# Forms of an input made by VectorE alone over three gate tiles, more convolution taps inside the attention, and the last pair's products in another order

## The chip, the cores and the metric

The kernel runs on one core of a Trainium2 chip. A core has a matrix engine (TensorE, PE in the profile, with its weight loads shown as PEld), a vector engine (VectorE, DVE), a scalar engine (ScalarE, ACT), a general engine (GpSimd, POOL) and a queue that issues DMAs (SyncE, SP). The metric is the device time of one launch, in microseconds (us), as a median of runs. Time before: 1506.61 us, median of 3 runs (1505.62 to 1508.06).

## The reference

One step of a streaming encoder layer. 1024 prompt frames and 32 sample frames (1056 columns in all, width 1024) are normalised, projected into nine column ranges of one matrix, and go through two branches that are mixed by gates:

```python
h = rmsnorm(x, norm_g)                      # (1056, 1024)
q, k, v, logf, ga, ua, ub, gb, ma, mb = column ranges of h @ w_in
q, k = per-head rmsnorm;  logf = log_sigmoid(logf + b_f);  c = cumsum(logf)
o = softmax(q k^T + c_q - c_k, causal) v    # 16 heads of 64; sample frames see 512 cached keys
u = ua * sigmoid(ub)
conv = causal depthwise convolution of u, 31 taps per channel, + b_dw
ya = (o * silu(ga)) @ w_pa
yb = (silu(layernorm(conv)) * silu(gb)) @ w_pb
m = sigmoid(ma) * ya + sigmoid(mb) * yb
y = x + m @ w_out
```

The keys, values, log gates and the last 30 rows of u are outputs too.

## The kernel before

Everything is laid out with channels on the 128 partitions and the 1056 columns along them, in eight tiles of 128 channels. All arithmetic is 32-bit: an operand is split into a high part (rounded, made on ScalarE) and a low part (the rest, made on VectorE or GpSimd), and a product is three matmuls, high by high, low by high, high by low. A projection tile is 128 output channels by three slices of 352 columns, 8 depth tiles each, so 24 steps of 3 matmuls (`steps`, L109 holds the matmuls). Its weights come by DMA as `raw` (L90), and are split into `wh` on ScalarE (L98) and `wl` on GpSimd (L101).

The stages follow one another:

1. Normalisation and transposition of the input, channels 0 to 3 of u, the values, then q and k (`qk`), whose rounded parts are stored to HBM in slices (L743 to L746, tiles `qh`, `ql`).
2. Attention, 16 heads by 8 blocks of 128 queries, plus four blocks for the sample frames. Only TensorE's order is as written; the other engines are ordered by a scheduler. The loop starts the scores three blocks ahead of the block whose weights are transposed (`turn`), and the weighted values come two blocks later (`values`). Between them `fill(4)` takes four steps of projections from a list, `FILLS`: u 4 to 7, ga 1 to 7, ma 0 to 5 (504 steps). They use one PSUM bank, `pq`.
3. The rest of ma (tiles 6 and 7), over which the forms (below) are made. From here to the end of the pairs TensorE, VectorE and ScalarE execute in the written order, in which `later(n, f)` places a piece of work n beats behind, a beat being a step of 3 matmuls.
4. gb and mb, 16 tiles in eight pairs. A pair of tiles is computed with seven products instead of eight (`Pair`, Strassen's scheme in Winograd's form, L1117 the matmuls, 24 per product). The input's halves in depth and columns are combined into the forms `xf` (three of them: index 1, 2 and 0) and a fourth, called `third` in the code, which is written over the input's own high and low parts once those are no longer needed as they were. The weights are combined per pair into `sa` and `sb` by VectorE (`made`, L1091 to L1099) and split (L1077 ScalarE, L1080 GpSimd). Seven products go to four PSUM tiles a, b, c, d; products 4, 5 and 6 reuse a, c and d once they have been evicted (`evac`, L1127 to L1145; product 0 and 4 on ScalarE, the others on VectorE).
5. The attention's output times silu(ga), called halves here (`a_half`, eight of them: two loads, an activation, a product, a high and a low part), then the projection pa, the convolution's layernorm beside it, pb and out.

The convolution is 31 taps per channel tile: the first on ScalarE, thirty on VectorE (L273, 240 in all). They stand in a list, `taps`. At each beat `pace["credit"]` grows by a rate and taps are taken while the credit allows; evictions and `made` charge it. The rates are `R_A` = 0.12 in the attention and `R_S` = 0.17 in the pairs; the gate tiles of stage 3 start with a credit of -9. At the beginning of the last pair whatever is left is issued at once, and the memory of the convolution is given to the tiles of the halves:

```python
            elif i == 0:
                pump(len(taps))
                pcv.close()
                pap = ExitStack()
                bg = pool("bg", 5, stack=pap, side="right")
            elif i in (3, 4):
                later(2, lambda i=i: (a_half(2 * i - 6), a_half(2 * i - 5)))
```

The forms in stage 3 are made so: GpSimd adds the high and low part of two input tiles (`form_adds`, L1015), VectorE adds a third, and subtracts (L1033, L1035, L1040), ScalarE rounds (L1022), VectorE makes the low parts (L1025). Two of the four tiles of form 0 and half of `third` are made during pair 0 (`fourth_adds`, `third_sums`, `third_form`, `third_low`, L1172 to L1177).

## Time and profile before

| | |
|---|---|
| median of 3 runs | 1506.61 us (1505.62 to 1508.06) |
| the profiled execution: time, span | 1510.4 us, 1508.6 us |
| granted clock, mean | 0.959 |
| TensorE busy | 1386.0 us, 92% |
| VectorE busy | 996.0 us, 66% |
| ScalarE, GpSimd busy | 653.5 us and 652.6 us, 43% each |
| DMA | 201.28 MB, 133 GB/s over the span |

Busy times of the profile are unions of an engine's instructions. The slices are fortieths of the span, 37.7 us each, and a digit is a tenth. In rows with "x", the number behind it counts instructions; in groups the three parts after the count are busy time, mean ns of one, and idle time before it with the engine and line that ended it. A wait row says who waited for whom: total, times, longest.

### The profile page before, as it was taken

Reading aid. Unit: us, or ns where it says so; the run is one execution under the profiler, and the core shown is the slowest. Engines: PE = TensorE matmul, PEld = TensorE weight load, DVE = VectorE, ACT = ScalarE, POOL = GpSimd, SP = SyncE. Lnnn points to the kernel's source line nnn. Section 1 sums busy time; section 2 is a strip of 40 time slices with the busy share of each in tenths; the row PEclk is TensorE's granted clock in tenths of the full one; section 3 lists DMA queues with packets and bytes.
Section 4 is the critical chain, followed back from the end, with each engine's and each line's share of the span. In section 5 each row is a group of like instructions: output and inputs, shape, how many; then the busy total and the mean of one; then the engine's idle time right before and its main releaser. Section 6 shows DMA issues by size and latency. Waiting matters only on the chain.

```text
span 1508.6 us, 25287 instructions
## 1 busy us (share of the span) xinstructions
PE 1386.0 (92%) x9574; PEld 1339.5 (89%) x9574; DVE 996.0 (66%) x1348; ACT 653.5 (43%) x1310; POOL 652.6 (43%) x694
## 2 busy tenths in 40 slices
PE   8999999999999999999999996699970489999999
PEld 7999999998999999999999986699970478999999
DVE  6788788887726666767666676848999677433211
ACT  6333336665655555555555562322210365522100
POOL 3333346675744443443533334656730135545321
PEclk9999999999999999999999998799995689999999
DMA  4353423566344434544545321133310577734531
GB/s 169 115 178 113 160 88 126 172 178 203 140 144 120 143 103 137 154 120 121 155 114 155 110 77 66 48 114 122 103 53 14 201 242 257 235 128 143 161 106 49
DMA packets 107274, 201.28 MB, mean 133 GB/s; under 512 B 16080, under 2 KB 67152, under 8 KB 107152
## 3 DMA queue, kind: packets, MB, share of 16 engines
q1 hardware_dynamic: 107008, 199.60, 41.9%
q8 instruction: 76, 1.25, 0.4%
q14 instruction: 46, 0.38, 0.1%
q10 hardware_dynamic: 144, 0.07, 0.0%
HBM read 129.78 MB, written 69.84 MB: 132 GB/s over the span
## 4 chain that ended last, share of the span: by engine, by line
PE 79%; DVE 10%; DMA 4%; issue 3%; ACT 2%; POOL 1%; SPq 0%; DVEq 0%; POOLq 0%; ACTq 0%
PE pj L109 48%; PE ps L1117 9%; PE pjv L607 6%; DVE y L273 4%; PE ptr L971 4%; PE po L987 3%; PE po L988 2%; PE psS L943 2%; PE psS L944 2%; DMA s_ya<-sma 1%; DMA s_k<-qh 1%; POOL wl L101 1%; DVE t L1015 1%; PE psS L946 1%; DVE y L1358 1%
## 5 line engine op out<-in xcount | busy, mean ns | idle before, releaser
L109 PE MATMUL pj<-xh,wh 128*128 128x352 f32 (+3 forms) x1152 | 387.0, 336 | 14.9 <-ACT t L765 14.4
L109 PE MATMUL pj<-xl,wh 128*128 128x352 f32 (+3 forms) x1152 | 373.2, 324 | 0.2 <-DVE xl L455 0.2
L273 DVE SCALAR_TENSOR_TENSOR y<-u,vec_t,y 128x1086 f32<-128x1086 f32 x240 | 367.0, 1530 | 8.0 <-ACT y L270 5.1
L109 PE MATMUL pj<-xh,wl 128*128 128x352 f32 (+3 forms) x1152 | 372.2, 323 | 0.1
L101 POOL TENSOR_TENSOR wl<-raw,wh 128x384 fp32r<-128x384 f32 (+1 forms) x210 | 242.5, 1183 | 193.8 <-ACT wh L98 171.9
L109 PEld LDWEIGHTS pj<-xh,wh 128*128 128x128 f32 x1152 | 218.3, 189 | 19.2 <-ACT t L765 16.1
L109 PEld LDWEIGHTS pj<-xh,wl 128*128 128x128 f32 x1152 | 218.9, 190 | 0.6 <-POOL wl L101 0.5
L109 PEld LDWEIGHTS pj<-xl,wh 128*128 128x128 f32 x1152 | 217.8, 189 | 1.4 <-DVE xl L455 1.4
L954 POOL TENSOR_SCALAR P<-P,nm 128x128 f32<-128x128 f32 (+7 forms) x128 | 99.6, 778 | 220.9 <-DVE nm L953 179.5
L109 PE MATMUL pj<-ah,wh 128*128 128x352 f32 x768 | 187.8, 327 | 6.6 <-ACT wh L98 6.6
L1117 PE MATMUL ps<-xh,wh 128*128 128x264 f32 x256 | 76.7, 300 | 74.0 <-DVE t L1145 65.3
L109 PEld LDWEIGHTS pj<-ah,wh 128*128 128x128 f32 x768 | 136.1, 192 | 7.3 <-ACT wh L98 7.2
L948 DVE TENSOR_REDUCE nm<-psS 128x1 f32<-128x128 f32 (+7 forms) x128 | 96.7, 756 | 56.1 <-PE psS L946 52.1
L109 PE MATMUL pj<-ah,wl 128*128 128x352 f32 x384 | 125.7, 327 | 8.1 <-POOL wl L101 8.0
L975 ACT CAST pth<-ptr 128x512 fp32r<-128x512 f32 (+1 forms) x192 | 88.8, 481 | 91.0 <-PE ptr L971 90.7
L976 DVE TENSOR_TENSOR ptl<-ptr,pth 128x512 fp32r<-128x512 f32 (+1 forms) x192 | 103.5, 552 | 30.0 <-ACT pth L975 27.1
L1117 PEld LDWEIGHTS ps<-xh,wh 128*128 128x128 f32 x256 | 51.7, 202 | 74.7 <-issue 65.5
L98 ACT CAST wh<-raw 128x1024 fp32r<-128x1024 f32 x70 | 73.4, 1048 | 93.2 <-PE pj L109 85.4
L951 ACT ACTIVATE P<-psS,nm 128x128 f32<-128x128 f32 (+7 forms) x128 | 95.3, 745 | 29.9 <-DVE nm L948 25.6
L744 POOL TENSOR_TENSOR ql<-qn,qh 128x352 fp32r<-128x352 f32 (+1 forms) x48 | 56.6, 1179 | 72.4 <-ACT qh L743 56.4
L971 PE MATMUL ptr<-ident,P 128*128 128x128 f32 x576 | 85.4, 275 | 1.3 <-DVE ptl L976 1.3
L109 PEld LDWEIGHTS pj<-ah,wl 128*128 128x128 f32 x384 | 73.8, 192 | 10.0 <-POOL wl L101 9.9
(245 smaller groups left out, 3040.6 us busy)
## 6 DMA issues: line engine op xcount, KB each, us to landing
raw<-wf SPq DMA_DIRECT2D x88, 512.0 KB
s_v<-vb SPq DMA_DIRECT2D x32, 256.0 KB
QB<-s_q SPq DMA_DIRECT2D x32, 256.0 KB
KB<-s_k SPq DMA_DIRECT2D x32, 256.0 KB
V<-s_v SPq DMA_DIRECT2D x16, 512.0 KB
kT<-qn SPq DMA_DIRECT2D x8, 528.0 KB
s_ga<-t SPq DMA_DIRECT2D x24, 176.0 KB
s_ma<-t SPq DMA_DIRECT2D x24, 176.0 KB
```

The costliest lines, as they stand in the source:

```text
L98: nc.scalar.copy(wh, raw)
L101: nc.gpsimd.tensor_sub(wl[:, k0:k1, :], raw[:, k0:k1, :], f32(wh[:, k0:k1, :]))
L109: nc.tensor.matmul(ps, a[:, kt, :], b(kt, sl), start=(first and n == 0), stop=(last and n == N - 1))
L273: t = nc.vector.scalar_tensor_tensor(y, u[:, i:i + CW], w, y, op0=ALU.mult, op1=ALU.add)
L607: nc.tensor.matmul(ps[:, :VC], a, b, start=(n == 0), stop=(n == 23))
L948: nc.vector.tensor_reduce(nm[:, 0:1], ps[:, :nb, :w], axis=AX.XY, op=ALU.max, negate=True)
L951: nc.scalar.activation(P[:, :nk].rearrange("p (b w) -> p b w", b=nb), ps[:, :nb, :w], AF.Exp, bias=nm[:, 0:1], accum_out=nm[:, 1:2])
L954: nc.gpsimd.tensor_scalar(P[:, :nk], P[:, :nk], nm[:, 2:3], 1.0, op0=ALU.mult, op1=ALU.mult)
L971: nc.tensor.transpose(pt[:, 128 * j:128 * j + 128], P[:, 128 * (4 * u + j):128 * (4 * u + j) + 128], ident)
L975: nc.scalar.copy(pth[:, js, qo], p3)
L976: nc.vector.tensor_sub(ptl[:, js, qo], p3, f32(pth[:, js, qo]))
L1117: nc.tensor.matmul(ps[:, c, :HC], a[:, k, :], x, start=(i < 4 and kt == 0 and n == 0), stop=(kt == 3 and n == 2), skip_group_check=(i >= 4))
```

## The change

It has four parts.

**Taps.** `R_A` goes to 0.18 and `R_S` to 0.27; stage 3 starts with a credit of -24 and pair 0 takes 3 instead of 8 off it.

**Gate tiles and forms.** ma 6 and 7 join `FILLS` (552 steps). A block with index 7 of each head isn't followed by filler. What is left of the list when the attention ends is run then, in the written order, with its PSUM tiles taken from `pq` and the attention's `psT` in turn. Over these steps all forms, the fourth tiles and `third` too, are made by VectorE and ScalarE; GpSimd makes none. `third` is kept in the tiles `sb` and `raw`, which are made larger for it.

**The last pair.** Its products come in the order 0, 1, 2, 3, 5, 6, 4. Halves 0 to 5 are loaded into the tiles `sa`, `sb` and the two `raw` and made between the products; halves 6 and 7 follow in the old way. The weights of pa's first tile are loaded beside product 6.

**Smaller ones.** Three buffers in place of two for `qh` and `ql`; the first head's load stands behind the last key projection; `ones` lies in another pool.

```diff
-R_U, R_V, R_QK, R_S, R_A = 0.25, 0.17, 0.19, 0.17, 0.12
+R_U, R_V, R_QK, R_S, R_A = 0.25, 0.17, 0.19, 0.27, 0.18
...
-         ("ma", 0), ("ma", 1), ("u", 7), ("ma", 2), ("ma", 3), ("ma", 4), ("ma", 5)]
+         ("ma", 0), ("ma", 1), ("u", 7), ("ma", 2), ("ma", 3), ("ma", 4), ("ma", 5),
+         ("ma", 6), ("ma", 7)]
...
-            qh = tp.tile([128, CH], F32R, name="qh", tag="qh")
-            ql = tp.tile([128, CH], F32R, name="ql", tag="ql")
+            qh = tp.tile([128, CH], F32R, name="qh", tag="qh", bufs=3)
+            ql = tp.tile([128, CH], F32R, name="ql", tag="ql", bufs=3)
...
+    class FillBanks:
+
+        n = 0
+
+        def tile(self, *a, **k):
+            self.n += 1
+            if "drain" not in sides or self.n % 2:
+                return pq.tile(*a, **k)
+            return psT.tile([128, 512], F32, name="pj", tag="T")[:, :CH]
...
-    def form_adds(j):
-        part[j] = x32(nc.gpsimd, j, 1), x32(nc.gpsimd, j + 4, 1)
-
-    def form_sums(j, fourth):
-        b12, b22 = part[j]
+    def form_sums(j):
+        b12 = x32(nc.vector, j, 1)
         b11 = x32(nc.vector, j, 0)
         nc.vector.tensor_sub(b11, b12, b11)
         high_of(1, j, b11)
+        b22 = x32(nc.vector, j + 4, 1)
+        nc.vector.tensor_sub(third[j], b22, b12)
         nc.vector.tensor_sub(b22, b22, b11)
         high_of(2, j, b22)
         part[j] = b11, b22
-        if fourth:
-            b21 = x32(nc.vector, j + 4, 0)
-            nc.vector.tensor_sub(b21, b21, b22)
-            high_of(0, j, b21)
-            part[j] = b11, b22, b21
+
+    def form_fourth(j):
+        b21 = x32(nc.vector, j + 4, 0)
+        nc.vector.tensor_sub(b21, b21, part[j][1])
+        high_of(0, j, b21)
+        part[j] += b21,
...
+    def third_high():
+        for j in range(4):
+            nc.scalar.copy(xh[:, j, HT:], third[j])
+
+    def third_low():
+        for j in range(4):
+            nc.vector.tensor_sub(xl[:, j, HT:], third[j], f32(xh[:, j, HT:]))
...
             b.turn()
-            fill(4)
+            if b.i < 7:
+                fill(4)
...
-    pace["credit"] = -9.0
+    pairs = [Pair(k) for k in range(len(SPAIRS))]
+    pace["credit"] = -24.0
...
+    later(39, first_loads)
     for j in range(4):
-        later(9 * j + 2, lambda j=j: form_sums(j, j < 2))
...
+        third[j] = t3[:, (j % 2) * HT:(j % 2) * HT + HT]
+        later(18 * j + 2, lambda j=j: form_sums(j))
+        later(18 * j + 7, lambda j=j: form_fourth(j))
+        later(18 * j + 12, lambda j=j: form_lows(j))
+    for i, at in enumerate((48, 57, 60)):
         later(at, lambda i=i: pairs[0].made(i))
-    later(44, lambda: third_sums((0, 1), nc.gpsimd))
-    for f in (6, 7):
-        for _ in gate_steps("ma", f, pjB):
-            pass
-    pB.close()
+    for _ in flow:
+        pass
...
+    def last_pair(n, i):
+        if n == 0:
+            pump(len(taps))
+            a_load(0, big_tile(srp, "sa"), big_tile(srp, "sb"))
+        elif n == 1:
+            a_load(1, big_tile(rss[0], "raw"), big_tile(rss[1], "raw"))
+        elif n == 2:
+            later(2, lambda: a_make(0))
+            later(3, lambda: a_load(2, big_tile(srp, "sa"), big_tile(srp, "sb")))
+            later(6, lambda: a_make(1))
+            later(7, lambda: a_load(3, big_tile(rss[0], "raw"), big_tile(rss[1], "raw")))
+        elif n == 4:
+            rawp[:] = [wp]
+            later(1, lambda: a_make(2))
+            later(2, lambda: a_load(4, big_tile(srp, "sa"), big_tile(srp, "sb")))
+            later(5, lambda: a_make(3))
+            later(6, lambda: a_load(5, big_tile(rss[0], "raw"), big_tile(rss[1], "raw")))
+        elif n == 5:
+            raw = load_raw(("pa", 0))
+            later(1, lambda: split.update({("pa", 0): split_w(raw)}))
+        elif n == 6:
+            later(1, lambda: a_make(4))
+            later(6, lambda: a_make(5))
...
         if k == 0:
-            pace["credit"] -= 8.0
...
+            pace["credit"] -= 3.0
+            later(1, third_high)
+            later(3, third_low)
+            later(9, lambda: p.made(3))
+            later(11, lambda: p.made(4))
+        for n, i in enumerate(range(7) if nxt else (0, 1, 2, 3, 5, 6, 4)):
             if nxt:
                 if i == 0:
-                    nxt.load()
+                    later(12 if k == 0 else 1, nxt.load)
...
-    for f in range(4, 8):
-        a_half(f)
+    for f in (6, 7):
+        a_load(f, big("a3"), big("g3"))
+        a_make(f)
```

`a_load` and `a_make` are the two halves of the old `a_half`: the two loads, and the rest.

More of the change, by code (lines that the diff above doesn't have):

```diff
@@ L84, in f32, with big_tile, whole @@
         return ap.bitcast(F32)
+    def big_tile(p, tag):
+        return p.tile([128, D if p is wp else TT], F32, name=tag, tag=tag, bufs=1)
+    def whole(t):
+        return t[:, :D].rearrange("p (k n) -> p k n", k=KT)
     def load_raw(key, offset=2000):
@@ L88, in load_raw @@
             rawp.append(rawp.pop(0))
-            raw = rawp[-1].tile([128, KT, 128], F32, name="raw", tag="raw", bufs=1)
+            raw = whole(big_tile(rawp[-1], "raw"))
             nc.sync.dma_start(raw, wf[WIDX[key]])
@@ L224, in shift_of @@
         shift = f32(yr)
-        ones = cvp.tile([128, 128], F32R, name="ones", bufs=1)
+        ones = vp.tile([128, 128], F32R, name="ones", bufs=1)
         nc.gpsimd.memset(f32(ones), 1.0)
@@ L807, in build @@
             heads = [Head(h) for h in range(H)]
+        qk("k", f)
         if f == 7:
             heads[0].load()
-        qk("k", f)
         qk("q", f)
@@ L834, in build @@
     pace["rate"] = R_A
-    psS = pool("psS", 2, stack=p2, space=PS)
-    psT = pool("psT", 3, stack=p2, space=PS)
+    psS = pool("psS", 2, stack=ppq, space=PS)
+    psT = pool("psT", 3, stack=ppq, space=PS)
     ap = pool("ap", 2, stack=p2, side="right")
+    class FillBanks:
[5 more added lines that the diff above has]
+            return psT.tile([128, 512], F32, name="pj", tag="T")[:, :CH]
+    pjF = FillBanks()
     def filler():
@@ L842, in filler @@
             if g == "u":
-                yield from u_steps(f, pq)
+                yield from u_steps(f, pjF)
             else:
-                yield from gate_steps(g, f, pq)
+                yield from gate_steps(g, f, pjF)
     flow = filler()
@@ L1046, in form_lows @@
             low_of(i, j, t)
-    def fourth_adds(j):
-        t2 = t528()
-        nc.gpsimd.tensor_add(t2, f32(xf[2][:, 0, j, :]), f32(xf[2][:, 1, j, :]))
-        part[j] = t2, x32(nc.vector, j + 4, 0)
-    def fourth_form(j):
-        t2, b21 = part[j]
-        nc.vector.tensor_sub(b21, b21, t2)
-        high_of(0, j, b21)
-    def fourth_low(j):
-        low_of(0, j, part.pop(j)[1])
+    third = {}
+    def third_high():
[4 more added lines that the diff above has]
+            nc.vector.tensor_sub(xl[:, j, HT:], third[j], f32(xh[:, j, HT:]))
     class Pair:
@@ L1089, in made @@
             elif i == 1:
-                self.sa = srp.tile([128, KT, 128], F32, name="sa", tag="sa")
+                self.sa = whole(big_tile(srp, "sa"))
                 nc.vector.tensor_add(self.sa[:, 4:, :], self.r1[:, :4, :], self.r1[:, 4:, :])
@@ L1096, in made @@
             elif i == 3:
-                sb = self.sb = srp.tile([128, KT, 128], F32, name="sb", tag="sb")
+                sb = self.sb = whole(big_tile(srp, "sb"))
                 nc.vector.tensor_sub(sb[:, :4, :], self.r0[:, :4, :], self.r1[:, :4, :])
@@ L1159, in build @@
                 ("a", 0, 1, part_of(4, 0)), ("c", 2, 1, part_of(4, 1)), ("d", 3, 0, form(0)))
-    third = {}
-    def third_sums(js, eng):
-        for j in js:
-            third[j] = x32(eng, j, 1), x32(nc.gpsimd, j + 4, 1)
-    def third_form(js):
-        for j in js:
-            t, b = third[j]
-            nc.vector.tensor_sub(t, b, t)
-            nc.scalar.copy(xh[:, j, HT:], t)
-    def third_low(js):
-        for j in js:
-            nc.vector.tensor_sub(xl[:, j, HT:], third[j][0], f32(xh[:, j, HT:]))
     slots = {}
@@ L1188, in big, with a_load, a_make @@
         return bg.tile([128, TT], F32, name=name, tag="big")
-    def a_half(f):
-        a, g = big("a3"), big("g3")
+    halves_of = {}
+    def a_load(f, a, g):
         nc.sync.dma_start(g, s_g["ga"][f])
         nc.sync.dma_start(a[:, :T], s_o[f, :, :T])
+        halves_of[f] = a, g
+    def a_make(f):
+        a, g = halves_of.pop(f)
         nc.scalar.activation(g, g, AF.Silu)
@@ L1224, in build @@
             heads[seq[n - 2].head.h + 1].load_v()
-    split["ma", 6] = split_w(load_raw(("ma", 6)))
+    split["ma", 5] = split_w(load_raw(("ma", 5)))
+    plan.extend([("ma", 6), ("ma", 7)])
     for b in seq[-2:]:
@@ L1228, in build @@
             b.values()
-    for _ in flow:
-        pass
-    plan.append(("ma", 7))
     p2.close()
@@ L1237, in build @@
     order.enter_context(tc.manual_schedule(engines={E.PE, E.DVE, E.Activation}))
+    sgs[:] = [pool("sgS")]
     ar = pool("ar", 1)
     pS = ExitStack()
-    sgs[:] = [pool("sgS", 1, stack=pS)]
-    rawp.extend(pool(f"rs{i}", 1, stack=pS) for i in range(2))
+    rss = [pool(f"rs{i}", 1, stack=pS) for i in range(2)]
     srp = pool("srp", 1, stack=pS)
@@ L1244, in build, with first_loads @@
     pup = pool("pup", 1, stack=pS)
-    pB = ExitStack()
-    pjB = pool("pjB", 3, stack=pB, space=PS)
+    sides["drain"] = True
     xf.extend(ar.tile([128, 2, 4, HT], F32R, name="xf", tag=f"s{i}") for i in range(3))
-    pairs = []
-    pace["credit"] = -9.0
-    def first_pair():
-        pairs.extend(Pair(k) for k in range(len(SPAIRS)))
+    pairs = [Pair(k) for k in range(len(SPAIRS))]
+    pace["credit"] = -24.0
+    def first_loads():
+        rawp[:] = rss[:1] + [wp] + rss[1:]
         pairs[0].load()
-    form_adds(0)
+    later(39, first_loads)
@@ L1256, in build @@
     for j in range(4):
-        later(9 * j + 2, lambda j=j: form_sums(j, j < 2))
-        if j < 3:
-            later(9 * j + 4, lambda j=j: form_adds(j + 1))
-        later(9 * j + 7, lambda j=j: form_lows(j))
-    later(13, first_pair)
-    for i, at in enumerate((25, 29, 31, 38, 40)):
-        later(at, lambda i=i: pairs[0].made(i))
-    later(44, lambda: third_sums((0, 1), nc.gpsimd))
-    for f in (6, 7):
-        for _ in gate_steps("ma", f, pjB):
-            pass
-    pB.close()
+        if j % 2 == 0:
+            t3 = big_tile(srp, "sb") if j == 0 else big_tile(rss[1], "raw")
@@ L1275, in build @@
         if k == 0:
-            pace["credit"] -= 8.0
-            later(1, lambda: third_form((0, 1)))
-            later(3, lambda: (third_low((0, 1)), third_sums((2, 3), nc.vector)))
-            later(8, lambda: third_form((2, 3)))
-            later(10, lambda: third_low((2, 3)))
-            for j in (2, 3):
-                later(8 * j, lambda j=j: fourth_adds(j))
-                later(8 * j + 5, lambda j=j: fourth_form(j))
-                later(8 * j + 8, lambda j=j: fourth_low(j))
-        for i in range(7):
+            pace["credit"] -= 3.0
[4 more added lines that the diff above has]
+        for n, i in enumerate(range(7) if nxt else (0, 1, 2, 3, 5, 6, 4)):
             if nxt:
                 if i == 0:
-                    nxt.load()
+                    later(12 if k == 0 else 1, nxt.load)
                 for m, (ai, at) in enumerate(((3, 2), (4, 1), (5, 2), (5, 4), (6, 2))):
@@ L1291, in build @@
                         later(at, lambda m=m: nxt.made(m))
-            elif i == 0:
-                pump(len(taps))
-                pcv.close()
-                pap = ExitStack()
-                bg = pool("bg", 5, stack=pap, side="right")
-            elif i in (3, 4):
-                later(2, lambda i=i: (a_half(2 * i - 6), a_half(2 * i - 5)))
+            else:
+                last_pair(n, i)
             for _ in p.product(i):
@@ L1302, in build @@
         beat()
-    raw = load_raw(("pa", 0))
-    split["pa", 0] = split_w(raw)
     order.close()
     pS.close()
+    pcv.close()
     rawp[:] = [wp]
@@ L1323, in build @@
     pjC = Banks3()
+    pap = ExitStack()
+    bg = pool("bg", 5, stack=pap, side="right")
     sg2 = pool("sg2", 4, stack=p3, side="right")
```

## The prediction

> **What bounds the kernel now.** I read the page first (busy shares, the 40 slices), then one table of windows cut at the stage borders, then TensorE's waits in the stages where it is not full, and the timeline of VectorE in the worst of them.

> ```profile
> PE 1386.0 (92%) x9574; PEld 1339.5 (89%) x9574; DVE 996.0 (66%) x1348; ACT 653.5 (43%) x1310; POOL 652.6 (43%) x694
> PE   8999999999999999999999996699970489999999
> DVE  6788788887726666767666676848999677433211
> ```

> TensorE is full nearly everywhere; the holes are around slices 25 and 26 and 30 to 34. The next table has, for each stretch, its length and the busy time of TensorE, its weight load, VectorE, ScalarE and GpSimd, then granted clock, DMA share and GB/s.

> ```profile
> 430.00:904.00 474.00, 472.55 (x3463) 443.55 (x3462) 310.32 (x598) 265.33 (x617) 185.03 (x325) 1.00 0.45 127
> 904.00:954.60 50.60, 32.01 (x198) 30.41 (x198) 35.64 (x42) 15.65 (x28) 22.38 (x18) 0.89 0.15 53
> 954.60:989.20 34.60, 26.61 (x168) 25.52 (x169) 26.87 (x26) 10.20 (x15) 26.05 (x17) 0.77 0.20 69
> 989.20:1112.00 122.80, 122.80 (x1010) 122.80 (x1010) 93.09 (x84) 32.69 (x39) 75.30 (x46) 1.00 0.34 114
> 1112.00:1186.20 74.20, 8.97 (x74) 8.76 (x72) 69.91 (x54) 1.76 (x2) 6.74 (x4) 0.58 0.04 15
> 1186.20:1210.00 23.80, 16.17 (x97) 15.68 (x97) 14.15 (x18) 15.71 (x20) 6.28 (x5) 0.79 0.94 333
> 1210.00:1227.40 17.40, 13.71 (x68) 13.34 (x69) 12.88 (x12) 7.25 (x7) 8.02 (x5) 0.72 0.74 267
> ```

> Attention (430 to 919, its last matmul below) and pairs 1 to 6 (989 to 1112) are TensorE's. Four places are not: the last two gate tiles with the forms, pair 0, the last pair, and the halves before the pa projection. What TensorE waits for there (from 900 to 980, then from 1100 to 1320), and VectorE's timeline in the last pair:

> ```profile
> 919.03 0.28 PE L988 MATMUL po<-ptl,V 128*128 128x256 f32 x1
> PE pj L109 <- ACT t L765: 14.4, 3, 10.0
> PE ps L1117 <- ACT xh L1173: 5.4, 1, 5.4
> PE ps L1117 <- DVE t L1145: 65.3, 1, 65.3
> 1109.91 28.44 DVE L273 SCALAR_TENSOR_TENSOR y<-u,vec_t,y 128x1086 f32<-128x1086 f32 x19
> 1140.76 39.44 DVE L273 SCALAR_TENSOR_TENSOR y<-u,vec_t,y 128x1086 f32<-128x1086 f32 x27
> 1227.43 1.48 DVE L1401 SCALAR_TENSOR_TENSOR sma<-sma,pj 128x352 f32<-128x352 f32 x3 [0.93 <-PE pj L109]
> ```

> The 65.3 us are the finding: at the last pair the kernel empties the list of convolution taps, 46 remain, and the eviction that product 3 needs stands behind them on VectorE.

> **The change, part by part.** Units first: a fill step is 3 matmuls of 352 columns, six pairs take 122.8 us.

> ```profile
> 411.61 3.82 PE pj L109 x24
> 430.00:904.00 474.00, 69.87 (x50) 1.00 0.45 127
> 989.20:1112.00 122.80, 44.03 (x26) 1.00 0.34 114
> L273 DVE SCALAR_TENSOR_TENSOR y<-u,vec_t,y x240: 1329/1350/3540, 53.0 to 1178.9; 128x1086 f32<-128x1086 f32 x120
> PE ptr L971 <- DVE ptl L976: 1.3, 1, 1.3
> PE pst L726 <- ACT sqh L716: 2.9, 1, 2.9
> PE pst L727 <- DVE sql L719: 1.0, 3, 0.5
> ```

> (The second and third rows are the taps alone in two windows; the last three are TensorE's waits, the largest of 430 to 920 and all of 100 to 430.) A step is 3.82/8 = 0.48 us, a pair 122.8/6 = 20.5, a product 2.9, a tap 1.35 alone.

> *Where the taps go.* By the instruction order of the changed program, VectorE has 120 taps before attention, as now; then 70 in attention (now 50), then 1, 11, 11, 10, 11, 6, 0, 0 counted from one pair's second eviction to the next. The list is empty when the last pair begins. So the flush goes.

> *Query and key stage* (third qh/ql buffer, head load behind the key projection): TensorE waits 3.9 us there in all. Bounds 0 and -3.9; I take **-2**.

> *Attention.* Filling skips each head's last block: by the rates 476 of 552 steps are done inside, against 504, so 28 steps (13.4 us) move behind attention, at no price, since TensorE is full in both places. Twenty more taps bring VectorE from 310.3/474 = 65% to about (310.3 - 69.9 + 70 x 1.4)/460 = 74%. Cover for them is the three blocks of run-ahead, which now lets TensorE wait 1.3 us at most; without that cover each tap would cost its 1.35. Where no filler stands between a last block's eight transposes and the next transposes, the PSUM bank must be drained within one values step, and a tap can be in the way, 16 times. Bounds: -1.3 (the one stall, near 905, gets filler again) and +16 x 1.35 - 1.3 = +20; I take **+2**, as today's 50 taps expose nothing.

> *Drain and forms.* Behind attention now come 48 steps (23.0 us) and pair 0 (20.5 us) in 989.2 - 919.3 = 69.9 us: 26.4 lost. After: 76 steps, 36.5 us, over forms made by VectorE alone: 11 operations per tile of four, 44, and 2 for the pair's weights. Their prices now:

> ```profile
> L1015 DVE TENSOR_TENSOR t<-xh,xl 128x528 f32<-128x528 f32 x8 | 11.9, 1502 | 0.0
> L1025 DVE TENSOR_TENSOR xf<-t,xf 128x528 fp32r<-128x528 f32 x10 | 6.6, 700 | 0.1
> L1015 POOL TENSOR_TENSOR t<-xh,xl 128x528 f32<-128x528 f32 x14 | 22.2, 1611 | 18.0 <-DMA s_o<-ot 16.1 <-DVE xf L1025 1.9
> ```

> The additions cost 1.50 beside GpSimd's own additions, the low parts 0.70 when GpSimd rests. With GpSimd's additions gone I take 0.66 to 0.70: 46 operations, 30 to 32 us, plus what GpSimd's weight subtractions (two gate tiles, the pair's first two splits, some 12 us) still hold up, 0 to 12: 30 to 44 us. Product 1, the first to read a form, is due at 39.4. The gate evictions on ScalarE stand in written order behind the forms' high copies, and TensorE has about 4 us of spare banks there. Loss 0 to 14 with pair 0's third form; I take 5: **-21.4**.

> *Pairs 1 to 5.* Here taps become dear.

> ```profile
> L273 DVE SCALAR_TENSOR_TENSOR y<-u,vec_t,y 128x1086 f32<-128x1086 f32 x25 | 43.8, 1751 | 1.4 <-ACT y L270 1.2
> L1092 DVE TENSOR_TENSOR sa<-sa,raw 128x512 f32<-128x512 f32 x7 | 10.9, 1553 | 0.2
> L1080 POOL TENSOR_TENSOR wl<-raw,wh 128x512 fp32r<-128x512 f32 x18 | 32.1, 1796 | 30.3 <-ACT wh L1077 30.3
> 1052.70 1.28 POOL L1080 TENSOR_TENSOR wl<-raw,wh 128x512 fp32r<-128x512 f32 x1
> L1145 DVE TENSOR_TENSOR t<-pu,ps 128x528 f32<-128x528 f32 x13 | 9.1, 700 | 13.3 <-PE ps L1117 13.3
> ```

> VectorE idles (122.80 - 93.09)/6 = 5.0 us per pair with 4.3 taps. A pair with 11 has 6.7 more: 9.0 us at 1.35, 11.7 at the 1.75 that taps take here beside GpSimd. Over by 4.1 to 6.8 us, in four pairs; the fifth, with 6 taps and a channel's sums, by about 2. TensorE tolerates a lag: the third product's bank is taken again two products (5.8 us) later, less the eviction, leaving 4.4. So 4 x 4.1 + 2 - 4.4 = 14 to 4 x 6.8 + 2 - 4.4 = 25. If in a full VectorE each of GpSimd's seven subtractions (1.28 alone, up to 1.80 here) blocks it entirely, 9.0 us per pair instead of about 3.3 now, it is up to 4 x 9.8 + 2 - 4.4 = 37. Nothing can make it a gain, since TensorE is full there; if the lag is absorbed elsewhere it is 0. Taps in a row took 28.44/19 = 1.50, so I stay above the middle: **+25**, range 0 to 37.

> [...]

> *The last pair and the halves.* From 1112.0 to the first pa eviction at 1227.4 are 115.4 us now. After: seven products 20.5, pa's first tile 72 x 0.16 = 11.5. Beside them six halves are loaded and made, each in this chain, and 1.06 MB at the 333 GB/s of 1186 to 1210, 3.2 us:

> ```profile
> L1194 ACT ACTIVATE g<-g x8: 1077/1085/1089, 1191.5 to 1221.6; 128x1056 f32<-128x1056 f32 x8
> L1196 DVE TENSOR_TENSOR a<-a,g x8: 1246/1258/2043, 1192.6 to 1222.9; 128x1056 f32<-128x1056 f32 x8
> L1198 ACT CAST ah<-a x8: 1055/1074/1075, 1194.0 to 1224.1; 128x1056 fp32r<-128x1056 f32 x8
> L1199 DVE TENSOR_TENSOR ah<-a,ah x8: 1245/1258/2051, 1195.1 to 1225.2; 128x1056 fp32r<-128x1056 f32 x8
> ```

> A half is 1.1 + 1.3 + 1.1 + 1.3 = 4.8 us behind its load. Half 0 lands about 9 us into the pair (its buffer is the last sb, free at about 3, then SP's queue with sma and the shift row beside it), is made by 14, half 1 by 18. VectorE has the eviction of product 2 behind these two, and product 5, reordered to follow product 3, needs that bank at 11.7: it waits about 6 us. Product 6 waits 2 more for half 2. On SP the loads of halves 6 and 7 stand ahead of these and wait for the convolution's memory, that is for GpSimd's last sum of squares, with the pair's stores behind them; that ends a pair earlier, so I cost it at nothing (if late, up to 5 us). On GpSimd pa's first split follows the last pair's: 1.5. Sum 20.5 + 8 + 1.5 + 11.5 + 0.9 = 42; bounds 33 (no wait) and 62 (six loads and makes one behind another, 6 x 8, and their tail before pa). **115.4 - 42: -73**.

> Behind that, 281 us stay as they are, +-4: the layernorm's chain starts from pa's first tile as now.

> **Sum.** -2 + 2 - 21.4 + 25 - 73 = -69.4. The profiled execution has a span of 1508.6 and took 1510.4, 3.8 above the median of the runs, 1506.61. So span 1439, and for the median **1437 us**. Nothing is charged for the larger raw, sa and sb tiles or for the third form kept in them: the loads that reuse them wait for low parts that VectorE has made by then, or else the lag shows in the drain's 5.

> **Rivals.** (1) *The extra taps fit* in the pairs (loss 0 to 8, say 6, instead of 25): 1418. For it: the 5.0 us of idle time; against: 11 x 1.35 + 4 x 0.68 + 5 x 0.70 = 21 us of VectorE's own work in 20.5, before GpSimd blocks any of it. (2) *The last pair gives it back*: halves hold VectorE's queue so long that the products wait for each load, 62 us instead of 42, and the drain loses 14: 1466. For it: the DMA share of 0.94 once halves load. (3) *Attention becomes VectorE's*, slower than before: the 70 taps stand in the chain reduce, exp, transpose. It decides from 1437 up to 1507, 70 us, so each of the 70 taps must expose 1.0 us of its 1.35: about 1510. Against it: 50 taps expose nothing now, at 65% busy. (4) *The flush stays*, because the list isn't empty: about 1506 less 20; the instruction order excludes it but for a hidden wait.

> **How the numbers follow.** Forecast 0.62, fitting taps 0.15, last pair 0.16, attention 0.05, flush 0.02. 1410 to 1466 takes in the first three's bounds. Faster than 0.2% (about what a measurement can tell): 0.94; slower: 0.05; same: 0.01.

> **What the changed profile would show.** Right: no wait over 10 us for an eviction in the last pair; 11 taps per pair and TensorE below full for pairs 2 to 5, waiting for VectorE's evictions, VectorE over 95%; drain near 40 us; attention's TensorE still full. Wrong: pairs at 20.5 us (rival 1), waits on ah or on evictions of 20 us and more in the last pair (2), waits on ptl or P all through attention (3).

## The result, and the profile after

The changed kernel takes 1440.78 us, the median of 4 runs (1439.35 to 1442.86), against 1506.55 us for the kernel before (median of 4, 1505.62 to 1508.06): a ratio of 0.9564, 95% interval 0.9547 to 0.958. The profiled execution took 1439.35 us with a span of 1437.6 us, 71.0 less than the 1508.6 of before. From the page, the engines' busy shares and two of the rows of 40 slices (now 35.9 us each):

```profile
PE 1378.6 (96%) x9574; PEld 1334.5 (93%) x9574; DVE 984.4 (68%) x1354; ACT 653.9 (45%) x1310; POOL 640.6 (45%) x678
...
PE   8999999999999999999999999999889598999998
...
DVE  6787797897835677777877777959997568233211
```

Every engine does nearly the work that it did. The long hole of TensorE is gone; slices 28 to 33, counted from 0, hold several small ones. The stretches between the same stage borders, with the columns of the prediction's table (length, TensorE, its weight load, VectorE, ScalarE, GpSimd, granted clock, DMA):

```profile
432.30:896.30 464.00, 459.12 (x3393) 430.12 (x3392) 341.55 (x635) 267.14 (x618) 186.71 (x320) 1.00 0.44 124
896.30:938.80 42.50, 37.13 (x216) 36.84 (x216) 37.64 (x46) 15.52 (x28) 14.17 (x10) 0.92 0.25 88
938.80:959.30 20.50, 20.48 (x168) 20.48 (x169) 11.65 (x14) 7.92 (x11) 11.25 (x9) 1.00 0.43 152
959.30:1105.80 146.50, 128.50 (x1010) 126.36 (x1009) 135.49 (x115) 35.06 (x42) 84.11 (x45) 0.97 0.31 104
1105.80:1158.00 52.20, 35.75 (x238) 35.34 (x237) 25.28 (x28) 19.77 (x23) 12.47 (x10) 0.84 0.63 217
1158.00:1437.60 279.60, 270.57 (x1674) 267.91 (x1673) 102.70 (x133) 85.69 (x110) 112.80 (x98) 0.99 0.49 158
```

And what TensorE waits for from the end of the attention to the first evictions of pa (total, times, longest):

```profile
PE ps L1133 <- DVE t L1155: 17.7, 5, 8.2
PE pj L116 <- ACT t L1147: 8.3, 1, 8.3
PE ps L1133 <- DVE t L1157: 5.8, 2, 4.4
PE pj L116 <- ACT t L772: 4.9, 1, 4.9
PE ps L1133 <- DVE t L1161: 2.4, 2, 1.9
```

L1155, L1157 and L1161 are evictions of products 2, 3 and 5 or 6 on VectorE, L1147 that of product 4 and L772 a gate tile's on ScalarE. No wait is as long as the 65.3 us of before; instead evictions are late by a few us in many places. Set beside each other, with the span divided at the same borders (in us; the last columns are experiments, told below). e8, e10 and e11 are medians of four launches, the other experiments one launch each; a stage is read from one profile. In the runs that leave a stage as the changed kernel has it, the attention takes 463.6 to 465.3 us and the last pair 51.4 to 54.9 (e6, e7 and e12), so less than 2 us in the one and 3.5 in the other is not told from chance:

| stretch | before | after | e1 | e2 | e5 | e10 | e8 |
|---|---|---|---|---|---|---|---|
| to the first scores | 438.2 | 432.3 | 431.3 | 437.6 | 432.6 | 430.6 | 430.5 |
| attention | 481.1 | 464.0 | 463.0 | 486.2 | 469.2 | 463.6 | 470.1 |
| gate tiles behind it, pair 0 | 69.9 | 63.1 | 62.5 | 70.0 | 63.3 | 62.6 | 59.9 |
| pairs 1 to 6 | 122.8 | 146.5 | 122.6 | 151.1 | 122.6 | 146.7 | 122.6 |
| last pair to the first pa eviction | 115.4 | 52.2 | 137.1 | 44.5 | 48.1 | 45.4 | 41.9 |
| the rest | 281.2 | 279.6 | 278.8 | 278.8 | 280.2 | 281.2 | 280.4 |
| span | 1508.6 | 1437.6 | 1495.2 | 1468.2 | 1415.9 | 1430.0 | 1405.4 |

### The profile page after: what moved, and what is told of

Same layout as the page of the kernel before. It is cut to its first block, busy times and chain, and to the rows that moved or that the text cites. A ratio compares the mean times of both kernels' runs of the same rounds, so it can differ in the third digit from the quotient of the medians.

```text
span 1437.6 us, 25249 instructions
## 1 busy us (share of the span) xinstructions
PE 1378.6 (96%) x9574; PEld 1334.5 (93%) x9574; DVE 984.4 (68%) x1354; ACT 653.9 (45%) x1310; POOL 640.6 (45%) x678
## 5 line engine op out<-in xcount | busy, mean ns | idle before, releaser
L967 DVE TENSOR_REDUCE nm<-psS 128x1 f32<-128x128 f32 (+7 forms) x128 | 96.5, 754 | 41.8 <-PE psS L965 34.6
L751 POOL TENSOR_TENSOR ql<-qn,qh 128x352 fp32r<-128x352 f32 (+1 forms) x48 | 58.2, 1213 | 64.3 <-ACT qh L750 53.1
L1133 PE MATMUL ps<-xf,wh 128*128 128x264 f32 x384 | 75.2, 291 | 6.0 <-DVE t L1157 5.8
L1006 PE MATMUL po<-pth,V 128*128 128x256 f32 x320 | 80.3, 286 | 0.0
```

The lines of the kernel that those rows point to most:

```text
L967: nc.vector.tensor_reduce(nm[:, 0:1], ps[:, :nb, :w], axis=AX.XY, op=ALU.max, negate=True)
L1006: nc.tensor.matmul(po[:, :256], V[:, j, :], pth[:, j, :], start=(j == 0), stop=False)
L1133: nc.tensor.matmul(ps[:, c, :HC], a[:, k, :], x, start=(i < 4 and kt == 0 and n == 0), stop=(kt == 3 and n == 2), skip_group_check=(i >= 4))
```

## The experiments

**The tap rates, taken away and alone.** Two runs make a table of two by two with the kernels before and after. e1 is the changed kernel with the old rates:

```diff
-R_U, R_V, R_QK, R_S, R_A = 0.25, 0.17, 0.19, 0.27, 0.18
+R_U, R_V, R_QK, R_S, R_A = 0.25, 0.17, 0.19, 0.17, 0.12
```

> The changed kernel with the two old rates, 0.12 in the attention and 0.17 in the pairs, everything else as changed. In its instruction order 47 taps lie in the attention, 16 in the pairs, and 57 are issued when the last pair begins. Theory (the gain is the flush, and the pairs pay for the taps): pairs 1 to 6 come back from 146.5 to about 123 us, and the last pair waits some 57 x 1.47 = 84 us behind its eviction, less the 8 us that it waits anyway and the 8 us before pa, which the halves' loads now spend beside the flush: 1441 - 24 + 84 - 16 = about 1485 us. Rival (the gain is in the forms and the halves, and the rates only move taps about): about 1441, within 10.

It took 1496.97 us. TensorE's waits in its last pair:

```profile
PE ps L1133 <- DVE t L1161: 81.4, 1, 81.4
PE ps L1133 <- DVE t L1155: 10.1, 1, 10.1
```

The flush is back, longer than before (81.4 us against 65.3), and pairs 1 to 6 are TensorE's again. So the rates are worth 56 us here, net of what they cost in the pairs; the rival falls. The theory's figure was 12 us too low: the last pair's other waits are not spent beside the flush, they come on top of it (10.1 us in the pair, and 7.7 before pa). e2 is the reverse, the kernel before with the new rates (0.27 and 0.18) as its only edit:

> The kernel before with the two tap rates of the change (0.27 in the pairs, 0.18 in the attention) and nothing else. By the instruction order 75 taps lie in the attention, then 6, 11, 9, 12, 7 in pairs 1 to 5, and none is left for the last pair. Theory (the rates carry most of the gain, and cost it again in the pairs): the last pair falls from 74 to about 21 us, pairs 1 to 6 grow by some 20 us through GpSimd, attention is unchanged: about 1473 us, between 1465 and 1480. Rival (taps are free wherever VectorE has idle time on the average): pairs stay at 123 us, and the time is about 1452.

It took 1469.98 us, in the theory's range, but not by its parts: the attention, which was to stay, grew by 5.1 us for 25 more taps (0.20 each), and pairs 1 to 6 by 28.3 rather than some 20. Two of its stretches, pairs 1 to 6 and the last pair up to pa's first eviction:

```profile
993.80:1144.90 151.10, 133.84 (x1010) 132.58 (x1009) 127.64 (x107) 33.47 (x42) 86.77 (x49) 0.91 0.34 118
1144.90:1189.40 44.50, 34.20 (x238) 33.13 (x238) 27.64 (x30) 21.57 (x22) 12.96 (x8) 0.88 0.60 210
```

Against the 1506.6 of before, the rates alone bring 36.6 us, all the rest alone 9.6, both 65.8. The rest alone brings so little because it lengthens the flush: with the old rates 47 taps lie in the attention and 16 in the pairs, against 50 and 24 in the kernel before (none lies between them in either), so 57 instead of 46 are left. The second row was a surprise: with the flush gone, the old form of the last pair takes 44.5 us, and the new one 52.2.

**GpSimd in the pairs.** e3 takes GpSimd's weight subtractions out of the pairs; ScalarE copies instead, so the low parts of gb's and mb's weights are left out.

```diff
-                    nc.gpsimd.tensor_sub(wl[:, k:k + 4, :], src[:, k:k + 4, :], f32(wh[:, k:k + 4, :]))
+                    nc.scalar.copy(wl[:, k:k + 4, :], src[:, k:k + 4, :])
```

> The changed kernel, but the low parts of the pairs' weights are not computed: ScalarE copies the weights in their place (1.05 us per 1024 columns on an engine that is busy 35 of 146.5 us there), and GpSimd does nothing in the pairs but the convolution's squares. The products are computed with these copies, so the output leaves out the exactness of gb and mb. Theory (VectorE is held up by GpSimd's instructions, one engine at a time): taps fall from 1.72 to about 1.40 us, VectorE needs 11 x 1.3 + 4 x 0.65 + 5 x 0.65 = 20 us per pair, and pairs 1 to 6 take 123 to 128 us instead of 146.5: about 1418 to 1423. Rival (VectorE's own work is too much, GpSimd doesn't matter): pairs 1 to 6 stay at 142 us and more, total at 1436 or above.

It took 1415.26 us, a little below the theory's range. Over pairs 1 to 6, the stretch and two of VectorE's groups (busy time, mean ns of one) in e3:

```profile
958.93:1081.89 122.96, 122.80 (x1010) 122.62 (x1009) 107.42 (x115) 55.14 (x81) 7.23 (x4) 1.00 0.37 125
```

```profile
L280 DVE SCALAR_TENSOR_TENSOR y<-u,vec_t,y 128x1086 f32<-128x1086 f32 x50 | 69.4, 1389 | 1.4 <-ACT y L277 0.7
...
L1155 DVE TENSOR_TENSOR t<-pu,ps 128x528 f32<-128x528 f32 x6 | 4.2, 698 | 0.1
```

The same groups in the changed kernel:

```profile
L280 DVE SCALAR_TENSOR_TENSOR y<-u,vec_t,y 128x1086 f32<-128x1086 f32 x50 | 84.5, 1689 | 0.8
...
L1155 DVE TENSOR_TENSOR t<-pu,ps 128x528 f32<-128x528 f32 x6 | 4.2, 697 | 0.1
```

With the same 50 taps, VectorE's busy time falls from 135.5 to 107.4 us, and the pairs return to TensorE's 123. A tap, which reads two tensors in SBUF, is 0.30 us dearer beside GpSimd (1689 ns against 1389); the eviction, with one operand in PSUM, costs the same (697 and 698). No wait of TensorE in the pairs of either kernel is for GpSimd itself. So the 23.7 us that the pairs lost are GpSimd's hold on VectorE and what follows from it, and 50 taps would fit without it. Two instructions in the trace of before agree with the theory's "one engine at a time": the weight sum L1092 took 0.69 us at 952.4, with GpSimd at rest, and 1.68 and 1.66 us at 1042.9 and 1063.3, where it began while a GpSimd subtraction ran and ended 0.55 us after that one's end.

**The taps elsewhere.** e5 has the same number of taps, but more of them inside the attention: tiles of u earlier in the list of fillers, so that their taps exist in time, and the rates turned round. 98 taps lie in the attention (70 in the changed kernel) and 22 in the pairs.

```diff
-R_U, R_V, R_QK, R_S, R_A = 0.25, 0.17, 0.19, 0.27, 0.18
+R_U, R_V, R_QK, R_S, R_A = 0.25, 0.17, 0.19, 0.18, 0.25
...
-FILLS = [("u", 4), ("ga", 1), ("ga", 2), ("ga", 3), ("u", 5), ("ga", 4), ("ga", 5), ("ga", 6), ("u", 6), ("ga", 7),
-         ("ma", 0), ("ma", 1), ("u", 7), ("ma", 2), ("ma", 3), ("ma", 4), ("ma", 5),
+FILLS = [("u", 4), ("ga", 1), ("ga", 2), ("u", 5), ("ga", 3), ("ga", 4), ("u", 6), ("ga", 5), ("ga", 6), ("ga", 7),
+         ("u", 7), ("ma", 0), ("ma", 1), ("ma", 2), ("ma", 3), ("ma", 4), ("ma", 5),
```

> The changed kernel with u 5, 6 and 7 earlier in the list of fillers, the attention's rate at 0.25 and the pairs' at 0.18: 98 taps lie in the attention (70 in the changed kernel), 22 in the pairs (50), none is left at the last pair. Theory (attention is TensorE's and hides taps, the pairs don't): pairs 1 to 6 fall from 146.5 to about 124 us, attention grows by no more than 6: about 1422 us. Rival (attention is at the edge, each further tap costs its time there): attention grows by 28 x 1.35 = 38, total about 1456.

It took 1417.66 us. Attention, and pairs 1 to 6:

```profile
432.60:901.80 469.20, 460.69 (x3394) 431.42 (x3392) 378.40 (x667) 268.91 (x620) 196.99 (x322) 1.00 0.45 123
...
965.10:1087.60 122.50, 122.50 (x1010) 122.50 (x1009) 89.31 (x84) 34.85 (x43) 75.20 (x45) 1.00 0.40 137
```

28 taps more cost the attention 5.2 us, 0.19 each, at 81% of VectorE; 28 fewer save the pairs 23.9 us, 0.85 each. The rival (attention becomes VectorE's) falls here too.

**The forms by VectorE alone.** e6 gives the additions `b12` and `b22`, two of the four per form tile, back to GpSimd, and leaves their place.

```diff
-        b12 = x32(nc.vector, j, 1)
+        b12 = x32(nc.gpsimd, j, 1)
...
-        b22 = x32(nc.vector, j + 4, 1)
+        b22 = x32(nc.gpsimd, j + 4, 1)
```

> The changed kernel with two of the three additions per form tile back on GpSimd (8 operations in all). [...] Rival (VectorE is the bound there, so help by GpSimd shortens it, and only the 4.9 us wait for the gate eviction behind the forms' high copies counts): 1435 to 1441.

It took 1440.23 us, where I had estimated 1445 to 1449, with 4 to 8 us more behind the attention: in the trace of before an addition takes 1.61 us on GpSimd, against 0.70 on VectorE at 947.5, where GpSimd rests. Its stretch behind the attention, and TensorE's wait there:

```profile
895.80:941.00 45.20, 37.30 (x217) 36.42 (x216) 33.22 (x38) 15.69 (x28) 20.84 (x16) 0.92 0.24 83
```

```profile
PE pj L116 <- ACT t L772: 7.3, 3, 4.9
```

The stretch grows by 2.7 us (45.2 against 42.5), less than the 4 to 8 estimated, and the total does not show it, because this run came to the first scores 1.5 us sooner; by the total alone the rival would hold. In the nine runs with the changed kernel's forms the stretch takes 42.0 to 42.8 us, so the 2.7 are no chance. So that VectorE makes all the forms is worth 2.7 us here. What else shortened this part is the order: 72 steps of TensorE stand beside the forms, which are done before pair 0 but for the writing of `third`, where before there were 31 steps and a fourth of the forms fell into pair 0. No run parts this from the rest.

**The small parts.** e7 undoes the third buffers of `qh` and `ql` and the place of the first head's load, e12 the buffers alone.

```diff
-            qh = tp.tile([128, CH], F32R, name="qh", tag="qh", bufs=3)
-            ql = tp.tile([128, CH], F32R, name="ql", tag="ql", bufs=3)
+            qh = tp.tile([128, CH], F32R, name="qh", tag="qh")
+            ql = tp.tile([128, CH], F32R, name="ql", tag="ql")
...
-        qk("k", f)
         if f == 7:
             heads[0].load()
+        qk("k", f)
```

> The changed kernel with two buffers for qh and ql again and the first head's load ahead of the last key projection. Theory (these two small parts are what brought the first scores forward from 438.2 to 432.3 us, more than TensorE's visible waits for sqh and sql): first scores at 438, time 1446. Rival (the scores start earlier for another reason, such as the order of taps): first scores at 432 to 433, time 1441.

> The changed kernel with two buffers for qh and ql again; the first head's load stays behind the last key projection. It parts the two halves of e7, which together moved the first scores from 432.3 to 439.7 us and put 2.7 us of waiting before sqh and 2.7 before sql. Theory (the buffers do it: a slice's copies wait for the store of the slice two before): first scores at 436 us or later, with waits of 2 us or more for sqh or sql. Rival (the place of the head's load does it, since its transfers stand ahead of the stores on SP's queue): first scores at 431 to 433, waits as in the changed kernel, 1.2 us in all.

e7 took 1451.31 us with the first scores at 439.7, e12 1445.26 us with the first scores at 437.1. TensorE's waits from 100 to 440 us, first of e7, then of e12:

```profile
PE pst L734 <- DVE sql L726: 3.5, 3, 2.7
PE pst L733 <- ACT sqh L723: 2.7, 1, 2.7
```

```profile
PE pst L733 <- ACT sqh L723: 2.6, 1, 2.6
```

The buffers carry 4.8 of the 7.4 us between 432.3 and 439.7, the head's load the other 2.6 with the second 2.7 us wait. Kernels alike up to this point differ by 2 us here (430.5 to 432.6), so the parting is rough; that the buffers count is not in doubt, since the 2.6 us wait is back (e12's theory asked for 436 or later and a wait of 2 us or more). The totals say less: the kernel before took 1511.4 us beside e12 and 1508.0 beside e7, and 2.7 us of e7's total lie in its last pair (54.9 us), which it leaves alone.

**The last pair.** Three runs. e4 keeps the new order but lets the evictions of products 2 and 3 go ahead of halves 0 and 1, and that of product 4 ahead of half 5 (a beat is a step; the loads of later halves move along):

```diff
         elif n == 2:
-            later(2, lambda: a_make(0))
...
-            later(6, lambda: a_make(1))
...
+            later(11, lambda: a_make(0))
...
+            later(19, lambda: a_make(1))
...
         elif n == 4:
...
-            later(1, lambda: a_make(2))
...
-            later(5, lambda: a_make(3))
...
+            later(5, lambda: a_make(2))
...
+            later(9, lambda: a_make(3))
...
         elif n == 6:
             later(1, lambda: a_make(4))
-            later(6, lambda: a_make(5))
+            later(11, lambda: a_make(5))
```

> The changed kernel with the halves of the last pair placed behind the evictions that products 5, 6 and pa wait for: half 0 behind the eviction of product 2, half 1 behind that of product 3, half 5 behind that of product 4. Theory (these evictions stand behind halves that wait for their loads): the wait of 8.2 us before product 5 falls under 1 us, that of 8.3 us before pa falls to about 3, and the time from the pair's start to pa's first eviction falls from 52.2 to about 40: about 1429 us. Rival (the loads and makes of the halves are the bound there, and the waits only move): 52 to 50 us, 1439 to 1441, with the same time now spent waiting for ah.

It took 1433.04 us, and 47.6 us from the start of the pair to pa's first eviction, where 40 had been expected. TensorE's waits in this stretch:

```profile
PE pj L116 <- ACT t L1147: 11.0, 1, 11.0
PE ps L1133 <- DVE raw L1198: 2.2, 1, 2.2
```

The wait before product 5 is gone, though product 6 now waits 2.2, and the one before pa grew from 8.3 to 11.0: the last product ends 23.0 us into the pair rather than 31.6, but half 4's copy, still ahead of product 4's eviction on ScalarE, begins at 32.4 as it did. So 4.6 us came of the 12 expected, and for the rest the rival holds: the wait moved to the next eviction. e9 takes the other part of the change back, the order:

```diff
-        for n, i in enumerate(range(7) if nxt else (0, 1, 2, 3, 5, 6, 4)):
+        for n, i in enumerate(range(7)):
```

> The changed kernel with the last pair's products in the order 0 to 6 again. Product 4 then covers the time in which the bank of product 2 is evicted behind the halves, but halves 4 and 5 are written where form 0 lay, which product 6 reads, now the last. Theory (the new order costs more than it brings): the wait before product 5 falls from 8.2 to under 5 us and the first matmul of pa comes no later behind the last product, time 1436 to 1439. Rival (the new order pays, because it frees the form's memory one product earlier): pa's first tile starts 3 us or more later, time 1443 or above.

It took 1442.34 us. The wait before product 5 fell to 3.4, and pa began directly behind the last product as the theory said; but then its second slice waited for a bank, that of an eviction on VectorE:

```profile
PE pj L116 <- DVE t L1161: 10.3, 1, 10.3
```

Its waits add up to 16.6 us, those of the changed kernel to 16.5, and pa's first eviction comes 53.1 us behind the start of the pair against 52.2. Neither the theory (1436 to 1439) nor the rival (1443 or more) has this time. So the order by itself is worth nothing that can be measured; it chooses which eviction stands behind the halves. e10 undoes the whole part: order, and halves as before (0 to 3 beside products 3 and 4, from the convolution's memory, 4 to 7 and pa's first weights behind the pair).

```diff
...
-            else:
-                last_pair(n, i)
+            elif i == 0:
+                pump(len(taps))
+                pcv.close()
+                pap = ExitStack()
+                bg = pool("bg", 5, stack=pap, side="right")
+            elif i in (3, 4):
+                later(2, lambda i=i: (a_half(2 * i - 6), a_half(2 * i - 5)))
...
```

> The changed kernel with the last pair and the halves as in the kernel before: products in the order 0 to 6, halves 0 to 3 made beside products 3 and 4 from tiles in the memory of the convolution, halves 4 to 7 and the weights of pa's first tile behind the pair. Theory (with the flush gone, making halves between the products costs more than it brings): as in the run with the rates alone, where it was 44.5 us from the start of the last pair to the first pa eviction against 52.2 in the changed kernel and 323.3 to the end against 331.8, so 1432 to 1434 us. Rival (the halves beside the products pay, and the run with the rates alone is short there for a reason of its own): 1441 or more.

It took 1432.7 us, the median of 4 runs (1430.92 to 1435.64; 0.9498 of before, 0.9475 to 0.9521): 8 us less than the changed kernel. Its largest waits of TensorE from 1103 to 1150 us:

```profile
PE pj L116 <- ACT wh L105: 5.4, 1, 5.4
PE pj L116 <- ACT ah L1205: 2.5, 1, 2.5
```

No product waits over 0.4 us: the halves stand a product later in the order, behind the eviction of product 2, and pa waits for its weights instead. (In their own buffers they are not late for it: half 0 is copied 11.2 us into the pair, 13.1 in the changed kernel.) So the third part of the change, as written, cost about 7 us.

**Together.** e8 is e5 with the evictions first, half 4 behind product 4's eviction as well as half 5, and the first form sums three beats later:

```diff
-        later(18 * j + 2, lambda j=j: form_sums(j))
+        later(18 * j + 2 + 3 * (j == 0), lambda j=j: form_sums(j))
...
         elif n == 6:
-            later(1, lambda: a_make(4))
-            later(6, lambda: a_make(5))
+            later(11, lambda: a_make(4))
+            later(12, lambda: a_make(5))
```

> The changed kernel with three things together: the taps moved into the attention (as in e5, 1417.7 us), the halves placed behind the evictions (0 and 1 behind those of products 2 and 3, 4 and 5 behind that of product 4), and the first form sums three beats later, so that the gate eviction in front of which TensorE waits 4.9 us goes ahead of the high copies. Theory (the three gains add: 4 for the wait, 4.6 for the last pair): 1409, between 1405 and 1412. Rival (the chain of halves ends when it ends, and the wait moves to the next eviction): 1415 to 1418.

It took 1408.59 us (1406.44 to 1410.8, 4 runs), 0.9334 of before (0.9314 to 0.9353), the best kernel of this study. Three of its stretches (behind the attention, pairs 1 to 6, last pair), and TensorE's longest wait in the last:

```profile
900.60:940.00 39.40, 35.32 (x218) 34.17 (x216) 37.70 (x46) 15.12 (x27) 13.74 (x10) 1.00 0.26 92
...
960.50:1083.10 122.60, 122.60 (x1011) 122.60 (x1010) 89.45 (x84) 34.85 (x43) 75.34 (x45) 1.00 0.40 136
1083.10:1125.00 41.90, 34.97 (x238) 33.52 (x237) 23.85 (x27) 18.12 (x19) 9.76 (x8) 0.92 0.63 211
```

```profile
PE pj L116 <- ACT t L1147: 5.5, 1, 5.5
```

The gains add. With half 4 out of the way as well, the last pair takes 41.9 us, against 48.1 in e5, whose last pair is the changed kernel's: the idea of halves between the products pays, by 3.5 to 4.3 us over the old form (45.4 in e10, 46.2 in e11), once the evictions stand further ahead. Not all do: the 5.5 us wait is for product 4's eviction, which still stands behind half 3's copy and a weight split on ScalarE. e11 confirms it by the last pair and halves of e10 in the place of e8's:

> As e8, but with the last pair and its halves as in the kernel before instead of the evictions first. Theory (the old form of the last pair is the better one once no taps are left to flush): the last pair begins at about 1083.5 us, and 323.3 us from there to the end of the span as in the run with the rates alone make 1408.5; between 1404 and 1411, and below e8. Rival (evictions first had already repaired the new form): no faster than e8.

It took 1412.84 us (1412.12 to 1413.62), 4 more than e8, with 46.2 us in this stretch. The theory falls, the rival holds.

## Why the prediction was right, and where its steps were off

The forecast was 1437, the kernel took 1440.78. The sum was -69.4 us of span, the measured sum -71.0, but three terms were off, in both directions.

- **Query and key stage**: -2 predicted, -5.9 measured, outside the bounds. The bound was made of TensorE's visible waits (3.9 us). Of these 2.7 went; e7 and e12 show that the buffers and the load do carry 7.4 us, more than the waits that they bring back. The rest is slower matmuls. Two windows from the start to the first scores, before and after, and one of before that begins in its 2.9 us wait (its clock is 0.50):

```profile
0.00:438.20 438.20, 430.08 (x2883) 419.62 (x2884) 331.48 (x385) 222.60 (x480) 216.76 (x190) 0.99 0.46 151
0.00:432.30 432.30, 427.03 (x2883) 417.42 (x2884) 330.08 (x385) 222.81 (x480) 219.07 (x189) 1.00 0.47 153
...
352.70:359.50 6.80, 5.91 (x19) 5.63 (x20) 5.93 (x7) 4.57 (x11) 6.78 (x7) 0.50 0.42 121
```

  The same 2883 matmuls keep TensorE busy 3.0 us less, and it idles 2.8 less. The bound had left out what a wait does to the clock (last section).
- **Attention**: 2 predicted for 20 more taps, and what they cost is of that size. The stretch is 17.2 us shorter. My count of moved steps was wrong, and without effect on the sum: the rows of TensorE in the two attention stretches, before and after, are

```profile
L109 PE MATMUL pj<-xh,wh 128*128 128x352 f32 x514 | 176.5, 343 | 0.3 <-ACT u L321 0.2
```

```profile
L116 PE MATMUL pj<-xh,wh 128*128 128x352 f32 x472 | 162.2, 344 | 0.9 <-DVE nm L972 0.7 <-ACT u L328 0.2
```

  with one such matmul per step. 41 steps left the attention (19.6 us; one of the 514 stands behind its last matmul), not 28: before, 17 of the 48 steps of the last two gate tiles had already been run before its last matmuls. 19.6 less 17.2 leaves 2.4 us for the taps, little more than runs alike differ by; e1, with 47 taps there, took 463.0. Rival 3 is refuted by a wide margin: e5 puts 28 more there at 0.19 us each.
- **Drain and pair 0**: by steps outside the attention, 31 before (14.8 us) and 72 now (34.4 us) beside pair 0's 20.5, the loss went from 34.6 to 8.2 us; 26.4 us of gain where -21.4 had been predicted (it had 26.4 lost before, since it counted all 48 steps as behind the attention, and 5 lost after). The mechanism named for the remaining loss was the right one: the 4.9 us wait is a gate eviction on ScalarE behind the forms' high copies, and e8 moves the copies and it is gone. VectorE's 37.6 us of work lies in the 30 to 44 estimated. What I gave most weight, the additions moved to VectorE, is worth 2.7 us (e6).
- **Pairs 1 to 5**: +25 predicted, +23.7 measured. VectorE is busy 92% of the time there (99% in pairs 2 to 5, where over 95% was foretold), and TensorE waits 17.8 us for its evictions. e3 shows the cause to be the one named. Rival 1 (the taps fit) would have been true with GpSimd at rest.
- **The flush and the last pair**: -73 predicted, -63.2 measured, the step that failed. The flush went as the instruction order said. The 42 us for the rest were 52.2: 32.0 us of products and pa, 16.5 of waits and 3.7 of slowed clock. The wait before product 5 was foreseen at 6 and is 8.2. The one before pa, 8.3 us, I put at 1.5 and on GpSimd; ScalarE's timeline shows what it is:

```profile
1138.15 1.07 ACT L1201 CAST ah<-sa 128x1056 fp32r<-128x1056 f32 x1 [3.39 <-DVE sa L1199]
1139.13 1.08 ACT L1197 ACTIVATE raw<-raw 128x1056 f32<-128x1056 f32 x1
1143.15 1.04 ACT L105 CAST wh<-raw 128x1024 fp32r<-128x1024 f32 x1 [2.95 <-DMA raw<-wf]
1144.11 1.07 ACT L1201 CAST ah<-raw 128x1056 fp32r<-128x1056 f32 x1
1145.08 0.59 ACT L1147 COPY t<-ps 128x528 f32<-128x528 f32 x1
```

  The eviction of product 4, 0.59 us of work, whose bank pa takes over, stands behind halves 4 and 5 and behind a weight split that waits 2.95 us for its load. I had followed the evictions that stand behind the halves on VectorE and not the one on ScalarE. The price stayed inside the bounds (33 to 62), and rival 2's mechanism is present at a part of its size.
- **The rest**: 0 predicted, -1.6 measured.

The forecast was right because its two large terms, the flush and GpSimd's hold on VectorE in the pairs, were right in mechanism; that it came within 4 us of the time is partly luck, since its errors in the first stage and behind the attention (-3.9 and -5.0) made up for the one in the last pair (+9.8).

## What to carry to other kernels

Work that may lie anywhere in an engine's written order is priced stage by stage: a tap cost 0.19 us inside the attention, 0.85 in pairs where GpSimd held VectorE up, and 1.4 in the flush (81.4 us for 57 in e1), so the best place for a tap is not simply the next one that has idle time on the average. Before large work is put into an engine's queue, list every eviction behind it, on every engine, and put the evictions first; with evictions behind the halves the new last pair lost 7 us to the old form (2 with the taps moved, e5 against e11), with the evictions further ahead it won 4. A sum of waits should be made with the clock that follows each of them (below).

## What the runs showed of the hardware that was not expected

The price of a TensorE wait is longer than the wait. In the changed kernel, three stretches from the 4.9 us gap on, then a gap of 4.4 us and what follows it:

```profile
896.30:901.20 4.90, 0.05 (x1) 0.05 (x1) 4.43 (x8) 1.98 (x4) 0.00 (x0) 0.83 0.61 214
901.20:905.00 3.80, 3.80 (x13) 3.80 (x14) 3.80 (x6) 1.58 (x2) 1.90 (x2) 0.50 0.13 50
905.00:910.00 5.00, 5.00 (x29) 5.00 (x28) 4.89 (x6) 1.58 (x3) 1.70 (x2) 0.86 0.41 140
...
1023.80:1028.30 4.50, 0.07 (x2) 0.02 (x1) 4.46 (x5) 0.65 (x1) 4.50 (x4) 0.73 0.08 30
1028.30:1031.60 3.30, 3.30 (x15) 3.30 (x16) 3.30 (x3) 0.39 (x1) 3.27 (x3) 0.50 0.21 82
```

After each the granted clock (the column ahead of the DMA share) is 0.50 for more than 3 us: 42 matmuls of 0.159 us (a third of a step), 6.7 us of work, took 8.8, so the 4.9 us gap cost 2.1 more. A shorter gap did it or not by where it fell. A wait of 2.35 us in front of a product left the clock at 1.00 in the changed kernel; the wait in front of the same product in e4, with 1.96 us of idle time in its window, halved it. Two neighbouring windows of each, first the changed kernel's, then e4's:

```profile
995.16:998.57 3.41, 1.69 (x14) 1.69 (x15) 3.41 (x4) 0.01 (x1) 0.00 (x0) 1.00 0.00 0
998.57:1001.98 3.41, 3.37 (x28) 3.17 (x27) 3.34 (x5) 1.05 (x1) 1.40 (x1) 1.00 0.33 126
...
993.57:996.98 3.41, 1.45 (x12) 1.45 (x13) 3.41 (x4) 0.25 (x1) 0.00 (x0) 1.00 0.00 0
996.98:1000.39 3.41, 3.41 (x18) 3.41 (x17) 3.34 (x5) 1.05 (x1) 1.17 (x1) 0.50 0.26 98
```

In pairs 1 to 6 this made 5.7 us of the 23.7 (TensorE busy 128.5 us for 122.8 us of work), in the last pair 3.7 of 52.2; the sum of the prediction had no such term. In e8 the waits behind the attention are split into pieces of at most 1.8 us, and there the clock is 1.00 throughout.
